# A diffusion backbone on one core: the first feed-forward projection of the second layer by seven products of sums of 2x2 blocks, mixed with the groups of the second projection

## The chip, the cores and the metric

The kernel runs on one core of a Trainium2 chip. The metric is the device time of one execution in microseconds (us), lower is better. The page calls the engines PE (TensorE, matrix products), PEld (its weight loads, which run beside it), DVE (VectorE), ACT (ScalarE), POOL (GpSimd) and SP (SyncE, which here issues transfers). Each engine works off its own instructions in the order in which the program has them, and semaphores hold an instruction back until what it reads is there.

## The reference, cut to what matters

The model has two layers. Each ends with a feed-forward block, and the change touches that of the second layer, in which 512 latent tokens remain (`l == 1`; the first layer also carries 256 context tokens):

```python
def sq_relu_mlp(h, w1, w2):
    return jnp.square(jax.nn.relu(h @ w1)) @ w2
...
    h2 = modulate(rmsnorm(x, g_ff[l]), sh2, sc2)
    x = x + gt2 * sq_relu_mlp(h2, w_ff1[l], w_ff2[l])
```

Here `h` is 512 x 1024, `w1` 1024 x 4096 and `w2` 4096 x 1024, all in 32-bit floats.

## The kernel before

Every 32-bit operand of a product is cut into a high part in the format fp32r and a low part, what is left over (`split`, lines 231 to 242: an ACT copy writes the high part `wh`, line 240; a subtraction, mostly on DVE, writes the low part `wl`, line 241). A product of two such operands takes three matmuls, high by high, high by low and low by high (`mmk`, line 260).

Tokens lie along the free dimension and channels along the 128 partitions. `w_ff1` comes in 32 tiles of 128 output channels, `w_ff2` in 32 tiles of 128 x 1024. The hidden width of 4096 is worked off in eight chunks of 512. In the second layer `ff1_first` computes the first projection of chunk 0 in two halves of 256 tokens; then for c = 1 to 7 `ff1(c)` computes the four tiles of chunk c (each 8 k-steps x 3 matmuls of 512 columns, `f<-h`), `act` applies relu (ACT, line 1226), squares on DVE (line 1228) and splits the result into `fh` and `fl`; and `ff2(c - 1)` runs the second projection of the chunk before: eight groups of 12 matmuls of 512 columns (`f<-fh`, `f<-fl`), one for each output tile `m`, each added into `x[m]` by one DVE instruction (line 1260, `xo<-f`). `ff2_last` does chunk 7 in halves of 256 tokens, and the final norm follows.

Weights come by DMA into `wraw`. `w_get` loads two tiles ahead and splits one tile ahead. Nothing is rescheduled: all engines run in the order in which the code issues instructions, and only background tasks (`spawn`, advanced by `tick`) are mixed in by a clock of estimated PE time. GpSimd takes the subtraction of every eighth weight tile here.

Of the kernel before, what the change touches and what calls it, by code (L numbers as in the profile page):

```python
# [17 lines left out]
DEPTH = 2  # L18
# [44 lines left out]
SLOTS_MIX = {3072: 6, 4096: 4}  # L63


class Slots:
# [46 lines left out]
class Net:  # L113
# [44 lines left out]
    def plan(self):  # L158
        d = self.d
        items = []  # L160

        def win(l, m):
# [12 lines left out]
        def ff1(l, c):  # L175
            for j in range(4):
                items.append((("ff1", l, 4 * c + j), d["w_ff1"][l, 4 * c + j], 1024))

        def ff2(l, c):
            for j in range(4):  # L180
                items.append((("ff2", l, c, j), d["w_ff2"][l, c, j], 1024))

        for l in range(DEPTH):
            for j in range(4):
                items.append((("v", l, j), d["w_v"][l, j], 1024))
            for m in (M_Q, M_K, M_Q + 1, M_K + 1, M_CONV + 2, M_CONV, M_Q + 2, M_K + 2, M_CONV + 3, M_CONV + 1,
                      M_Q + 3, M_K + 3, M_POOL, M_POOL + 1, M_FOUR, M_FOUR + 1):
# [6 lines left out]
            for c in range(1, 8):  # L194
                ff1(l, c)
                ff2(l, c - 1)
            ff2(l, 7)
        self.items = items
        self.n_dma = self.n_split = self.n_got = 0
        self.raw, self.wsp = {}, {}  # L200

    def anywhere(self, i):
        key = self.items[i][0]
# [2 lines left out]
    def w_advance(self, dma, split):  # L206
        nc, sb = self.nc, self.sb
        while self.n_dma < min(dma + 1, len(self.items)):
            i = self.n_dma
            t = sb.get([128, self.items[i][2]], F32, "wraw", self.anywhere(i))  # L210
            nc.sync.dma_start(t, self.items[i][1])
            self.raw[i] = t
            self.n_dma += 1
        while self.n_split < min(split + 1, len(self.items)):
            i = self.n_split
            eng = nc.gpsimd if i % self.pool_share == 0 or i < 4 else nc.vector
            self.wsp[i] = self.split(self.raw[i], "w", ph=self.anywhere(i), eng=eng)
            sb.free(self.raw.pop(i))
            self.n_split += 1

    def w_get(self, *key, split=1, dma=2):
        i = self.n_got
        assert self.items[i][0] == key, (self.items[i][0], key)
        self.n_got += 1
        if split == 1 and not self.in_attention and i + 1 < len(self.items) and self.items[i + 1][0][0] == "br":
            split = 2
        self.w_advance(i, i)
        self.w_advance(i + split, i + split)
        self.w_advance(i + split + dma, i + split)
        return self.wsp.pop(i)  # L230


# [882 lines left out]
    def mixer(self, l, ready, ready_ctx, between):  # L1115
        sb = self.sb
        wide = l < DEPTH - 1
        pairs, attn = [self.values(l, wide, ready, ready_ctx, between)], []
        attention = self.spawn(self.attend(l, wide, pairs, attn, PACE[l]))
        zs, us, up, four, pool, conv = [], [], [], [], [], []  # L1120
        threads = {}
        pairs.append(self.qk(l, 1, wide))
        zs.append(self.conv_in(l, wide, 0))
        pairs.append(self.qk(l, 2, wide))
        zs.append(self.conv_in(l, wide, 1))
        pairs.append(self.qk(l, 3, wide))
        self.pool_in(l, wide, up)
        self.four_in(l, wide, us)

        def attended():  # L1130
            self.join(attention)
            sb.free(*self.v)
            sb.close()
            sb.open(self.tc, SLOTS_MIX)
# [80 lines left out]
    def ff(self, l, ranges, groups, x, h, na, nb, after, near):  # L1215
# [17 lines left out]
        def ff1_first():  # L1233
            ws = [self.w_get("ff1", l, j, split=0 if j < 3 else 1) for j in range(4)]
            banks = [self.bank("f1") for _ in range(4)]
            for k in range(KT):
                self.until(*na, k)
                for w, b in zip(ws, banks):
                    self.mmk(w, 128 * k, h[k], groups[:1], (b,), k == 0, k == KT - 1)
            self.until(*nb, KT - 1)  # L1240
            hid = [act((b,), groups[:1]) for b in banks]
            for w, hl in zip(ws, hid):
                banks = self.proj(w, K8, h, groups[1:], "f1", need=nb)
                sb.free(*w)
                act(banks, groups[1:], hl)
            return hid
# [27 lines left out]
        def ff2_last(hid):  # L1274
# [15 lines left out]
                sb.free(*t)  # L1290
            after(1, ssq, last)

        self.pool_share = SHARES[2 + l]
        hid = ff1_first()
        for c in range(1, 8):
            nxt = ff1(c)
# [365 lines left out]
```

## Time and profile before

| | |
|---|---|
| median of 3 runs | 2151.26 us (2147.72 to 2151.81) |
| the profiled execution | 2151.51 us, of which 2149.7 us are the span on the core |
| PE busy | 2097.2 us, 98% of the span |
| DVE busy | 1378.7 us, 64% |
| ACT busy | 775.2 us, 36% |
| granted TensorE clock, mean | 0.993 |

PE is busy nearly throughout, so the time is read as the sum of PE's matmuls and of the few stretches in which it waits. A busy share of PE says nothing of its pace: matmuls overlap in the records, and the pace is read from where consecutive ones start. For DVE and ACT the share is an average, and what counts is whether a result is there when PE comes to it.

### The profile page before, as it was taken

To read this page: it belongs to the slowest core of one execution; us is meant where nothing else is said; L and a number is where in the kernel's file an instruction comes from. 1 tells how busy PE (TensorE), PEld (TensorE's weight loads), DVE (VectorE), ACT (ScalarE), POOL (GpSimd) and SP (SyncE) were. 2 spreads that over 40 slices of the span, in tenths; PEclk is the share of its full clock that TensorE was granted. 3 is DMA by queue.
4 is the path that set the end of the run, shared out by engine and by line. 5 is a ranking of instruction groups with operands and counts; after the bars stand their busy time and mean duration, and the time that the engine had idled before them with its cause. 6 is when DMAs were issued, how large, how long until landed. Compare 5 with 4: busy or idle time off the path is not lost. (4 is left out here: it accounts for less than half of the span.)

```text
span 2149.7 us, 29024 instructions
## 1 busy us (share of the span) xinstructions
PE 2097.2 (98%) x11700; PEld 1801.3 (84%) x11700; DVE 1378.7 (64%) x2234; ACT 775.2 (36%) x1258; POOL 451.4 (21%) x391
## 2 busy tenths in 40 slices
PE   8899999999999999999999999989999999999998
PEld 6688898888788888888888887878887898888887
DVE  6667658669876559868534365775986465544446
ACT  2455543223443342222112234565333334322333
POOL 2433220015442321212000023333100031000001
PEclk8999999999999999999999999999999999999999
DMA  8111112133344124446321121212332232232221
GB/s 306 44 55 59 55 54 91 50 114 122 118 131 152 71 99 166 165 165 248 109 69 59 60 89 55 69 46 101 121 101 86 98 109 99 97 108 89 88 98 50
DMA packets 62166, 218.36 MB, mean 102 GB/s; under 512 B 7248, under 2 KB 9312, under 8 KB 62032
## 3 DMA queue, kind: packets, MB, share of 16 engines
q1 hardware_dynamic: 45136, 155.21, 21.2%
q0 software_dynamic: 16896, 61.30, 8.3%
q8 instruction: 92, 1.51, 0.3%
q14 instruction: 42, 0.34, 0.0%
HBM read 212.29 MB, written 4.19 MB: 101 GB/s over the span
## 5 line engine op out<-in xcount | busy, mean ns | idle before, releaser
L241 POOL TENSOR_TENSOR wl<-wraw,wh 128x1024 fp32r<-128x1024 f32 x90 | 221.3, 2460 | 1205.2 <-ACT wh L240 956.8
L260 PE MATMUL f<-h,wh 128*128 128x512 f32 (+1 forms) x1600 | 388.7, 349 | 0.0
L260 PEld LDWEIGHTS f<-h,wh 128*128 128x128 f32 x1600 | 264.1, 189 | 41.9
L240 ACT ACTIVATE wh<-wraw 128x1024 fp32r<-128x1024 f32 x268 | 274.2, 1049 | 47.9 <-DVE wl L241 24.0
L241 DVE TENSOR_TENSOR wl<-wraw,wh 128x1024 fp32r<-128x1024 f32 x178 | 243.3, 1371 | 35.6 <-ACT wh L240 33.7
L260 PE MATMUL f<-h,wl 128*128 128x512 f32 (+1 forms) x800 | 243.9, 350 | 0.0
L260 PE MATMUL f<-fh,wh 128*128 128x512 f32 (+1 forms) x800 | 242.8, 349 | 0.0
L260 PE MATMUL f<-fh,wl 128*128 128x512 f32 (+1 forms) x800 | 242.5, 348 | 0.0
L260 PE MATMUL f<-fl,wh 128*128 128x512 f32 (+1 forms) x800 | 242.2, 348 | 0.0
L1260 DVE SCALAR_TENSOR_TENSOR xo<-f,mod,xo 128x512 f32<-128x512 f32 (+1 forms) x200 | 122.9, 640 | 126.7 <-PE f L260 126.6
L1226 ACT ACTIVATE ft<-f 128x512 f32<-128x512 f32 (+1 forms) x100 | 48.0, 510 | 431.5 <-PE f L260 431.5
L321 DVE CUSTOM_DVE_ANT_0 junk<-wm,silu,pp 128x1024 bf16<-128x1024 f32 x116 | 157.7, 1360 | 12.2 <-DMA wm<-w_mod 10.9
L260 PE MATMUL g<-h,wh 128*128 128x512 f32 x512 | 161.3, 393 | 0.0
L1228 DVE TENSOR_TENSOR ft<-ft 128x512 f32<-128x512 f32 (+2 forms) x72 | 54.4, 755 | 166.2 <-ACT ft L1226 166.2
L260 PEld LDWEIGHTS f<-h,wl 128*128 128x128 f32 x800 | 135.5, 189 | 20.7
L260 PEld LDWEIGHTS f<-fh,wh 128*128 128x128 f32 x800 | 134.9, 188 | 21.0 <-issue 0.2
L260 PEld LDWEIGHTS f<-fl,wh 128*128 128x128 f32 x800 | 134.7, 188 | 21.0 <-issue 0.2
L260 PEld LDWEIGHTS f<-fh,wl 128*128 128x128 f32 x800 | 134.7, 188 | 20.7
L260 PE MATMUL g<-hh,wl 128*128 128x512 f32 (+1 forms) x512 | 131.4, 337 | 1.1 <-DVE wl L241 1.1
L260 PE MATMUL g<-hh,wh 128*128 128x512 f32 (+1 forms) x512 | 131.6, 338 | 0.0
L260 PE MATMUL g<-hl,wh 128*128 128x512 f32 (+1 forms) x512 | 131.5, 338 | 0.0
L643 DVE SCALAR_TENSOR_TENSOR ca<-z,pp,ca 128x783 f32<-128x783 f32 (+1 forms) x120 | 121.0, 1009 | 1.9
(401 smaller groups left out, 3905.9 us busy)
## 6 DMA issues: line engine op xcount, KB each, us to landing
wraw<-w_ff SPq DMA_DIRECT2D x128, 512.0 KB, 3.5
wraw<-w_in SPq DMA_DIRECT2D x96, 512.0 KB, 3.5
wm<-w_mod POOLq DMA_DIRECT2D x80, 512.0 KB, 4.5
wm<-w_mod SPq DMA_DIRECT2D x16, 512.0 KB, 10.2
wraw<-w_out SPq DMA_DIRECT2D x16, 512.0 KB, 3.5
wraw<-w_v SPq DMA_DIRECT2D x8, 512.0 KB, 4.9
bias<-bias POOLq DMA_DIRECT2D x16, 256.0 KB, 2.9
wraw<-w_ba SPq DMA_DIRECT2D x8, 512.0 KB, 3.8
```

Of the source, the lines that this page charges most:

```text
L240: nc.scalar.activation(hi, src, AF.Copy)
L241: (eng or nc.vector).tensor_tensor(lo, src, hi.bitcast(F32), op=OP.subtract)
L260: self.nc.tensor.matmul(o[:, :t1 - t0], a[:, sl], b[:, t0:t1], start=start and a is wh and b is xh, stop=stop and a is wl)
L321: nc.vector.tensor_tensor_reduce(self.junk, w, self.silu[c], 1.0, b, OP.mult, OP.add, o)
L643: nc.vector.scalar_tensor_tensor(a[:, :n], zs[ct][:, j:j + n], w, a[:, :n], op0=OP.mult, op1=OP.add)
L1226: nc.scalar.activation(t[:, a - a0:e - a0], o[:, :e - a], AF.Relu)
L1228: nc.vector.tensor_tensor(t, t, t, op=OP.mult)
L1260: nc.vector.scalar_tensor_tensor(x[m][:, a:e], o[:, :e - a], self.modcol(l, int(a >= SEQ), 5, m), x[m][:, a:e], op0=OP.mult, op1=OP.add)
```

## The change

In the second layer the first projection of 13 of the 16 pairs of weight tiles (pairs 3 to 15; pairs 0 and 1 are chunk 0, and pair 2 stays as it was) is computed in another way. Weights of a pair and tokens are both cut in 2x2 blocks (two halves of the 1024 input channels by two output tiles, and by two halves of the 512 tokens). Instead of eight block products there are seven, P1 to P7, of sums and differences of blocks (Strassen's scheme in Winograd's form). Each product is 12 matmuls of 256 columns. The sums of the token side (T1 to T4) are formed once (`sums`), those of the weight side for every pair (`seven_weights`), and the results are combined while they leave the accumulators (`seven`, `square`). `ff_order` lays out by a fixed rule which product or second-projection group comes next, and `w_ahead` issues weight splits for all that comes within 6 us of PE time by that list, and loads for 12 us.

```diff
+SLOTS_MIX = {3072: 6, 4096: 4}, {3072: 2, 4096: 7}
+STRASSEN = (1,)
+PLAIN_PAIRS = 3
+SEVEN = "P1", "P6", "P7", "P5", "P2", "P4", "P3"
+SPLIT_US, LOAD_US, FF_LEAD = 6.0, 12.0, 5.6
...
+            for q in (2 * c, 2 * c + 1):
+                if q < PLAIN_PAIRS:
+                    a += [("plain", 2 * q + i, 0, 24 * us) for i in range(2)]
+                else:
+                    a += [("seven", q, j, 6 * us) for j in range(7)]
+            b = deque(("add", c - 1, m, 12 * us) for m in range(8))
+            total, more, ta, tb = sum(s[3] for s in a), sum(s[3] for s in b), 0.0, 0.0
+            for s in a:
+                while b and (ta - FF_LEAD) / (total - FF_LEAD) > (tb + 6 * us) / more:
+                    out.append(b.popleft())
+                    tb += 12 * us
+                out.append(s)
+                ta += s[3]
+            out += b
...
+        name = SEVEN[j]
+        if name == "P1":
+            src = a
+        elif name == "P6":
+            st["s1"], st["s2"] = (sb.get([128, 512], F32, "ws", ph=True) for _ in range(2))
+            nc.vector.tensor_tensor(st["s1"], c, e, op=OP.add)
+            src = st["s2"]
+            nc.vector.tensor_tensor(src, st["s1"], a, op=OP.subtract)
+        elif name == "P7":
+            src = c
+            nc.vector.tensor_tensor(src, a, c, op=OP.subtract)
...
+        else:
+            src = st["s1"]
+            nc.vector.tensor_tensor(src, b, st["s2"], op=OP.subtract)
+        w = sb.get([128, 2, 512], F32R, "w7", ph=True)
+        self.split(src, "w7", w[:, 0], w[:, 1])
...
+            for k in range(4):
+                v = sb.get([128, 4, 256], F32, "v7", ph=True)
+                for i in range(2):
+                    hi, lo = (t[:, :512].bitcast(F32).rearrange("p (a b) -> p a b", a=2) for t in h[k + 4 * i])
+                    nc.vector.tensor_tensor(v[:, 2 * i:2 * i + 2], hi, lo, op=OP.add)
+                    yield 0.7
+                for o, a, b in ((0, 1, 0), (1, 3, 1), (3, 3, 0), (2, 2, 3)):
+                    nc.vector.tensor_tensor(v[:, o], v[:, a], v[:, b], op=OP.subtract)
+                yield 1.0
...
+                    blocks[n].append(self.split(v[:, i], "T7", hi, lo))
+                    yield 0.6
...
+            b1, o1 = product(0)
+            nc.scalar.activation(u, o1, AF.Copy)
+            yield
+            b6, o6 = product(1)
+            nc.vector.tensor_tensor(u, o6, u, op=OP.add)
...
+            product(5)
+            nc.vector.tensor_tensor(t1[:, 0], o7, u, op=OP.add)
+            ps.free(b7)
+            nc.scalar.activation(t1, t1, AF.Relu)
+            square(t1, hid[1])
+            yield
+            product(6)
+            nc.vector.tensor_tensor(t0[:, 1], o5, u, op=OP.add)
+            ps.free(b5)
+            nc.scalar.activation(t0[:, 1], t0[:, 1], AF.Relu)
+            square(t0, hid[0])
...
+        def square(t, hl):
+            f = t.rearrange("p a b -> p (a b)")
+            nc.scalar.activation(f, f, AF.Square)
+            self.split(f, "f", hl[0], hl[1])
```

The order of the steps that `ff_order` gives for chunks 2 to 7 is the same each time: P1, P6, P7, P5, P2 of the first pair, add 0, P4, add 1, P3, then of the second pair P1, add 2, P6, add 3, P7, add 4, P5, add 5, P2, P4, add 6, P3, add 7 ("add m" is the second projection's group for output tile m, of the chunk before).

PE, in chunk 1, before: a tile of the first projection is 24 matmuls of 512 columns, of which these six are two k-steps (`h` with an odd number is the high part, with an even number the low part).

```order
L260 MATMUL f_1457_16119<-h_15603,wh_16075 128x512
L260 MATMUL f_1457_16119<-h_15604,wh_16075 128x512
L260 MATMUL f_1457_16119<-h_15603,wl_16076 128x512
L260 MATMUL f_1457_16119<-h_15605,wh_16075 128x512
L260 MATMUL f_1457_16119<-h_15606,wh_16075 128x512
L260 MATMUL f_1457_16119<-h_15605,wl_16076 128x512
```

PE, with the change, in chunk 2: the second half of product P6, from columns of `h` set aside for a token sum and the weight sum `w_3444`, and the first matmuls of group add 3.

```order
L1441 MATMUL f_1496_16684<-h_15615,w_3444_16619 128x256
L1441 MATMUL f_1496_16684<-h_15616,w_3444_16619 128x256
L1441 MATMUL f_1496_16684<-h_15615,w_3444_16619 128x256
L1441 MATMUL f_1496_16684<-h_15617,w_3444_16619 128x256
L1441 MATMUL f_1496_16684<-h_15618,w_3444_16619 128x256
L1441 MATMUL f_1496_16684<-h_15617,w_3444_16619 128x256
L364 MATMUL f_1498_16698<-fh_16078,wh_16611 128x512
L364 MATMUL f_1498_16698<-fl_16079,wh_16611 128x512
```

A product is half as wide as a matmul before, and first- and second-projection groups now alternate within a chunk.

DVE, over one chunk's end and the next one's start, before: the last two additions into `x`, then weight tiles `wl` alternate with the squaring (`ft`) and the low part (`fl`) of a finished tile.

```order
L1260 SCALAR_TENSOR_TENSOR xo_15446<-f_1473_16297,mod_103,xo_15446 128x512
L1260 SCALAR_TENSOR_TENSOR xo_15477<-f_1475_16311,mod_103,xo_15477 128x512
L241 TENSOR_TENSOR wl_16326<-wraw_16261,wh_16325 128x1024
L1228 TENSOR_TENSOR ft_16358<-ft_16358 128x512
L241 TENSOR_TENSOR fl_16357<-ft_16358,fh_16356 128x512
L241 TENSOR_TENSOR wl_16364<-wraw_16295,wh_16363 128x1024
```

DVE, with the change, at the same place: the combination after P4 (`ft_17064`) and the low part of its square, add 6 (`xo_15446`), the low part of the next P1's weights (`w_3581`), the two sums and the low part for P6 (`ws`, `w_3584`), the combination after P3 (`ft_17063`) and its low part, add 7 (`xo_15477`), and the difference (`wraw_17207`) and low part for the next P7 (`w_3607`).

```order
L1465 TENSOR_TENSOR ft_17064<-f_1532_17135,u_3552_17065 128x256
L345 TENSOR_TENSOR fh_17062<-ft_17064,fh_17061 128x512
L1364 SCALAR_TENSOR_TENSOR xo_15446<-f_1540_17239,mod_103,xo_15446 128x512
L345 TENSOR_TENSOR w_3581_17253<-wraw_17205,w_3581_17253 128x512
L294 TENSOR_TENSOR ws_17256<-wraw_17207 128x512
L296 TENSOR_TENSOR ws_17257<-ws_17256,wraw_17205 128x512
L345 TENSOR_TENSOR w_3584_17260<-ws_17257,w_3584_17260 128x512
L1471 TENSOR_TENSOR ft_17063<-f_1535_17169,u_3552_17065 128x256
L345 TENSOR_TENSOR fh_17060<-ft_17063,fh_17059 128x512
L1364 SCALAR_TENSOR_TENSOR xo_15477<-f_1543_17282,mod_103,xo_15477 128x512
L299 TENSOR_TENSOR wraw_17207<-wraw_17205,wraw_17207 128x512
L345 TENSOR_TENSOR w_3607_17304<-wraw_17207,w_3607_17304 128x512
```

The weights of the next chunk's first products now stand behind the combinations and additions of the chunk that ends.

ACT, with the change, over the same stretch: relu, square and high part of P4's result (`ft_17064`, `fh_17061`), the high parts for the next P1 and P6, relu, square and high part of P3's result, and the high part for P7.

```order
L1467 ACTIVATE ft_17064<-ft_17064 128x512
L1480 ACTIVATE ft_17064<-ft_17064 128x512
L344 ACTIVATE fh_17061<-ft_17064 128x512
L344 ACTIVATE w_3581_17253<-wraw_17205 128x512
L344 ACTIVATE w_3584_17260<-ws_17257 128x512
L1473 ACTIVATE ft_17063<-ft_17063 128x256
L1480 ACTIVATE ft_17063<-ft_17063 128x512
L344 ACTIVATE fh_17059<-ft_17063 128x512
L344 ACTIVATE w_3607_17304<-wraw_17207 128x512
```

Before, ACT had one relu and one high part for a finished tile, with DVE's squaring between them; now three ACT instructions follow each other between DVE's combination and DVE's low part.

## Rows read from the trace of the kernel before

**Rows 1.** The page's head, and the last chain (start us, us, what; matmuls counted).

```profile
span 2149.7 us, 29024 instructions
PE 2097.2 (98%) x11700; PEld 1801.3 (84%) x11700; DVE 1378.7 (64%) x2234; ACT 775.2 (36%) x1258; POOL 451.4 (21%) x391
...
1799.99 329.38 PE f L260 x1508
```

**Rows 2.** Windows: one chunk of the second layer's feed-forward, and a stretch of halves.

```profile
core 0: us, PE busy (x) PEld busy (x) DVE busy (x) ACT busy (x) POOL busy (x), PEclk, DMA share, GB/s
1849.32:1893.70 44.38, 44.38 (x195) 36.30 (x194) 21.75 (x24) 12.53 (x16) 2.40 (x1) 1.00 0.29 95
...
2116.00:2120.00 4.00, 4.00 (x36) 4.00 (x35) 2.42 (x5) 1.79 (x3) 0.00 (x0) 1.00 0.00 0
```

**Rows 3.** Timeline of PE: start us, us, what, count. Starts of groups give the pace.

```profile
1827.12 0.39 PE L260 MATMUL f<-fh,wh 128*128 128x512 f32 x1
...
1849.32 0.61 PE L260 MATMUL f<-h,wh 128*128 128x512 f32 x2
...
2114.96 0.28 PE L260 MATMUL f<-fh,wh 128*128 128x256 f32 x1
...
2120.65 0.27 PE L260 MATMUL f<-fh,wh 128*128 128x256 f32 x1
```

**Rows 4.** Groups of instructions, chunks 1 to 7: busy us, mean ns, idle before.

```profile
L240 ACT ACTIVATE wh<-wraw 128x1024 fp32r<-128x1024 f32 x58 | 57.8, 1045 | 0.0
L1260 DVE SCALAR_TENSOR_TENSOR xo<-f,mod,xo 128x512 f32<-128x512 f32 x55 | 41.2, 749 | 57.3 <-PE f L260 57.3
L241 DVE TENSOR_TENSOR fl<-ft,fh 128x512 fp32r<-128x512 f32 x28 | 19.4, 693 | 19.6 <-ACT fh L240 19.6
L240 ACT ACTIVATE fh<-ft 128x512 fp32r<-128x512 f32 x28 | 17.7, 633 | 21.2 <-DVE ft L1228 21.2
L241 DVE TENSOR_TENSOR fl<-ft,fh 128x256 fp32r<-128x256 f32 x1 | 0.4, 426 | 0.5 <-ACT fh L240 0.5
L240 ACT ACTIVATE fh<-ft 128x256 fp32r<-128x256 f32 x1 | 0.4, 418 | 0.5 <-DVE ft L1228 0.5
```

**Rows 5.** Timeline of DVE and of ACT in chunk 2.

```profile
1855.62 0.69 DVE L1228 TENSOR_TENSOR ft<-ft 128x512 f32<-128x512 f32 x1 [4.21 <-ACT ft L1226]
1857.01 0.69 DVE L241 TENSOR_TENSOR fl<-ft,fh 128x512 fp32r<-128x512 f32 x1 [0.70 <-ACT fh L240]
...
1874.60 1.23 DVE L241 TENSOR_TENSOR wl<-wraw,wh 128x1024 fp32r<-128x1024 f32 x1 [0.26 <-ACT wh L240]
1875.74 0.74 DVE L1260 SCALAR_TENSOR_TENSOR xo<-f,mod,xo 128x512 f32<-128x512 f32 x1
...
1856.34 0.63 ACT L240 ACTIVATE fh<-ft 128x512 fp32r<-128x512 f32 x1 [0.76 <-DVE ft L1228]
1856.88 1.05 ACT L240 ACTIVATE wh<-wraw 128x1024 fp32r<-128x1024 f32 x1
```

**Rows 6.** Timeline of PE: three of its waits, and what followed the longest.

```profile
1408.13 0.39 PE L915 MATMUL S<-qk,qw 128*128 128x256 f32 x1 [2.08 <-DVE PTl L967]
...
733.28 1.12 PE L428 MATMUL rstd<-diag,ones 128*128 128x512 f32 x2 [2.52 <-DVE diag L422]
...
1767.96 0.70 PE L428 MATMUL rstd<-diag,ones 128*128 128x256 f32 x2 [3.27 <-DVE diag L422]
1768.31 0.58 PE L260 MATMUL o<-br,wh 128*128 128x256 f32 x2
...
1772.10 0.45 PE L260 MATMUL o<-br,wh 128*128 128x256 f32 x2
```

**Rows 7.** Windows after three of those waits (columns as in Rows 2).

```profile
735.50:737.50 2.00, 2.00 (x11) 2.00 (x11) 1.87 (x2) 1.17 (x2) 2.00 (x2) 0.50 0.00 0
1408.20:1410.20 2.00, 2.00 (x11) 1.74 (x12) 1.04 (x5) 1.29 (x3) 0.00 (x0) 1.00 0.48 131
1770.00:1772.00 2.00, 2.00 (x11) 2.00 (x11) 1.86 (x1) 0.51 (x2) 2.00 (x1) 0.50 0.00 0
```

More of the change, by code (lines that the diff above doesn't have):

```diff
@@ L160, in plan @@
         items = []
+        self.when, self.sevens = {}, {}
         def win(l, m):
@@ L193, in plan @@
             ff1(l, 0)
-            for c in range(1, 8):
-                ff1(l, c)
-                ff2(l, c - 1)
+            if l in STRASSEN:
+                t = 0.0
+                for kind, a, b, us in self.ff_order(l):
+                    if kind == "plain":
+                        items.append((("ff1", l, a), d["w_ff1"][l, a], 1024))
+                    elif kind == "seven":
+                        items.append((("seven", l, a, b), d["w_ff1"][l, 2 * a + b] if b < 2 else None, 1024))
+                    elif b % 2 == 0:
+                        items.append((("ff2", l, a, b // 2), d["w_ff2"][l, a, b // 2], 1024))
+                    self.when[items[-1][0]] = self.when.get(items[-1][0], t)
+                    t += us
+            else:
+                for c in range(1, 8):
+                    ff1(l, c)
+                    ff2(l, c - 1)
             ff2(l, 7)
@@ L200, in plan, with ff_order @@
         self.raw, self.wsp = {}, {}
+    @staticmethod
+    def ff_order(l):
+        w = NTOK if l < DEPTH - 1 else SEQ
+        us = w / 2217.0
+        out = []
+        for c in range(1, 8):
+            a = []
+            for q in (2 * c, 2 * c + 1):
[12 more added lines that the diff above has]
+            out += b
+        return out
     def anywhere(self, i):
@@ L229, in w_get, with seven_weights, w_ahead, until @@
         self.w_advance(i + split + dma, i + split)
+        return self.wsp.pop(i)
+    def seven_weights(self, i, l, q, j):
+        nc, sb = self.nc, self.sb
+        st = self.sevens.setdefault((l, q), {})
+        if j < 2:
+            st["raw", j] = self.raw.pop(i)
+        a, b = (st["raw", 0][:, 512 * k:512 * k + 512] for k in range(2))
+        if j:
+            c, e = (st["raw", 1][:, 512 * k:512 * k + 512] for k in range(2))
+        name = SEVEN[j]
[9 more added lines that the diff above has]
+            nc.vector.tensor_tensor(src, a, c, op=OP.subtract)
+        elif name == "P5":
+            src = st["s1"]
+        elif name == "P2":
+            src = b
+        elif name == "P4":
+            src = e
+        else:
+            src = st["s1"]
+            nc.vector.tensor_tensor(src, b, st["s2"], op=OP.subtract)
+        w = sb.get([128, 2, 512], F32R, "w7", ph=True)
+        self.split(src, "w7", w[:, 0], w[:, 1])
+        if name == "P4":
+            sb.free(st["raw", 1])
+        if name == "P3":
+            sb.free(st["raw", 0], st["s1"], st["s2"])
+        return w
+    def w_ahead(self, *key):
+        i = self.n_got
+        now = self.when[key]
+        def until(us):
+            j = i
+            while j + 1 < len(self.items) and self.when.get(self.items[j + 1][0], now + us + 1.0) <= now + us:
+                j += 1
+            return j
+        split, load = max(until(SPLIT_US), i + 1), until(LOAD_US)
+        self.n_got += 1
+        assert self.items[i][0] == key, (self.items[i][0], key)
+        self.w_advance(i, i)
+        self.w_advance(split, split)
+        self.w_advance(max(load, split + 1), split)
         return self.wsp.pop(i)
@@ new lines, in square, with mixed @@
+        def square(t, hl):
+            f = t.rearrange("p a b -> p (a b)")
+            nc.scalar.activation(f, f, AF.Square)
+            self.split(f, "f", hl[0], hl[1])
+        def mixed():
+            hid = ff1_first()
+            t7 = self.spawn(sums())
+            nxt, gen = [], None
+            for kind, a, b, _ in self.ff_order(l):
+                if kind == "plain":
+                    w = self.w_ahead("ff1", l, a)
+                    banks = self.proj(w, K8, h, ranges, "f1")
+                    sb.free(*w)
+                    nxt.append(act(banks, ranges))
+                elif kind == "seven":
+                    if b == 0:
+                        self.join(t7)
+                        pair = [tuple(sb.get([128, SEQ], F32R, "fh", ph=True) for _ in range(2)) for _ in range(2)]
+                        nxt += pair
+                        gen = seven(a, pair)
+                    next(gen)
+                else:
+                    if b % 2 == 0:
+                        w2 = self.w_ahead("ff2", l, a, b // 2)
+                    ff2_one(a, b, w2, hid, ranges)
+                    if b % 2:
+                        sb.free(*w2)
+                    if b == 7:
+                        for t in hid:
+                            sb.free(*t)
+                        hid, nxt = nxt, []
+            for t in h:
+                sb.free(*t)
+            sb.free(*x7["keep"])
+            return hid
```

66 lines of the change are left out of this document (61 added, 5 removed).

## Prediction, written before the changed kernel ran

> **What bounds the kernel now.** The page comes first: PE is busy for 98% of the span and the chain that ended last is one unbroken run of feed-forward matmuls [rows 1]. Next come the windows over the second layer: a chunk of the feed-forward takes 44.3 us, PE is busy through all of it at a granted clock of 1.00, DVE is busy for 21.75 us of it and ACT for 12.5 [rows 2]. So this part is as long as PE's matmuls, and the two engines that prepare operands have about half their time free. The timeline gives PE's pace: from 1827.12 to 1849.32 lie 96 matmuls of 512 columns, 231 ns each; from 2114.96 to 2120.65 lie 48 of 256 columns (four groups of 12), 118.5 ns each [rows 3].
>
> **What the change takes off PE.** A pair of tiles is 2 x 24 = 48 matmuls of 512 columns, 48 x 0.2308 = 11.08 us. Seven products of 12 matmuls of 256 columns are 84 x 0.1185 = 9.95 us. That is 1.12 us for a pair and **14.6 us** for 13 pairs, if PE never waits.
>
> The weight loads rise from 48 to 84 for a pair. In the 256-column stretch PEld is busy without a break, yet the matmuls start every 118.5 ns [rows 2, 3]: the load is hidden there, and I charge nothing for it. [...]
>
> **What it puts on DVE and ACT.** Prices from rows: a DVE instruction of 512 columns 0.69 us, of 256 0.43, an addition into `x` 0.75; an ACT pass of 512 columns 0.63, of 256 0.42, of 1024 1.05 [rows 4]. If the next instruction waits for nothing it starts 0.08 to 0.09 us before the end, so that in a row DVE gives 0.61, 0.67 (addition) and 1.14 (weight tile of 1024) and ACT 0.54; a hand-over from DVE to ACT takes 0.03 and back 0.04 [rows 5]. No row has a combination that reads an accumulator at 256 columns; I take 0.43, bounded by 0.35 (0.43 in a row) and the 0.75 of an addition twice as wide.
>
> Per chunk of two pairs DVE has 14 low parts (8.5), 8 weight sums (5.2, some waiting for each other), 10 combinations (4.0), 4 low parts of results (2.4), 4 weight tiles (4.6) and 8 additions (5.4): 30.1 us. DVE works in order, and behind some of these it stands until ACT is through, with everything behind it: P6, P7 and P3 form a sum, ACT copies it, DVE subtracts (0.70 each); P4's result goes through three ACT passes before its low part (3 x 0.63 and hand-overs, 2.0), P3's through three as well (1.8). Per pair 5.9, per chunk 11.8. So DVE is taken up for 42 us, and PE's work in a chunk is 2 x 9.95 + 96 x 0.231 = 42.05. There is no slack left: any bunching makes PE wait, and the weights of all of the next seven steps stand behind it in DVE's queue.
>
> **Where it bunches.** I walk the rows of the order from a point at which DVE is idle and waits for PE, the end of add 5. From there DVE has to do, before PE can start the next chunk's P7: the addition (0.2 after PE's end, 0.67), a weight tile (1.14), P3's sum, ACT and low part (0.69, 0.70, 0.61), P4's combination, ACT and low part (0.43, 2.02, 0.61), addition (0.67), P1's low part (0.61), P6's two sums, ACT and low part (0.69, 0.72, 0.70, 0.61), P3's combination, ACT and low part (0.43, 1.81, 0.61), addition (0.67), P7's difference and ACT (0.69, 0.66). With 0.1 for PE to take it up this is **16.0 us**. PE meanwhile has P2, P4, add 6, P3, add 7, P1 and P6: 5 x 1.42 + 2 x 2.77 = **12.6 us**. So PE waits 3.4 us before each P7 of a chunk's first pair, and 0.5 in it for the low part. The lead of 6 us doesn't help, because it counts PE's clock at which DVE is to be handed the work, not when DVE reaches it.
>
> From the end of add 0 the same walk gives add 2's weights after 8.5 us (addition, P3's sum, ACT, two low parts, combination, 2.02 of ACT, low part, addition, weight tile), where PE comes to their low part after P4, add 1, P3, P1 and two matmuls, 7.5: 1.0. Then P6 of the second pair waits 0.2, and P7 1.3 (0.8 and 0.5). Sum per period: 3.9 + 1.0 + 0.2 + 1.3 = 6.4 us, a period of **48.5 us** against 44.3 before. Between add 0 of chunk 2 and add 0 of chunk 7 lie five periods: 32.2 us. After it chunk 7 still has 2.5, and the last groups wait some 1.5 for the result of the last P3.
>
> **The first chunk with the new products.** The token sums stand in DVE's queue in four bundles: 2 additions of 512 columns, 4 differences and 4 low parts of 256, some 4.6 us each, 18.5 together. Before P6 of pair 3 has its low part DVE must work off these, three weight tiles (3.4), the squares of pair 2 (2.6), three additions (2.0), P1's low part (0.6) and P6's sums (2.0): 29.1 us, and waits for ACT of about 3.8, from 1.9 us after the chunk's start (that is when `ff1_first` leaves DVE): **34.8 us**. PE is there after 11.08 + 4 x 2.77 + 1.42 and two matmuls = 23.8. So 11.1 us of waiting lie ahead of this point, most of it in one piece. The rest of the chunk, up to the first P7 of chunk 2, adds 5 more. Bounds: nothing, if the sums had been done in DVE's free time, and 18.5 plus that 5 if none of them were.
>
> **The clock.** [...] From 1768.31 to 1772.10 lie 18 matmuls of 256 columns in 3.79 us in place of 2.13: 1.66 us lost [rows 6]. Seven of the waits above are longer than 2.52 (one before P6 of pair 3, six before the first P7 of a chunk): 7 x 1.66 = 11.6 us.
>
> **The sum.** Waits 11.1 + 5 + 32.2 + 2.5 + 1.5 = 52.3; the clock 11.6; less 14.6: +49.3 us. The profiled execution took 2151.5, which is also within 0.3 us of the median: **2201 us**. GpSimd takes fewer weight tiles than before and loads are issued 12 us ahead, with DMA busy for 0.29 of a chunk [rows 2]; both I take as hidden, and a load late by its lead would show as DVE waiting for a DMA.
>
> **Rivals.**
> - *The lead covers it, faster.* The place is the stretch from add 5 to P7. If DVE's work and waits there come to at most 12.6 us in place of 16.0, a fifth less, DVE is there first and stays there; the token sums then fall into the 22 us that DVE has free in a chunk. Then PE only saves: 2151.5 - 14.6 = 2137. For it speaks that DVE's busy share alone, 30 of 42 us, is well below full; against it that the pauses for ACT are as plain in the trace as the work (0.70 in each `fl` [rows 5]). Chance 0.18.
> - *PE waits as worked out, but the clock holds or the waits are half as long.* The waits of 3.4 need only shrink by 0.9 to come to the row of 2.52. Without the clock's part it gives 2189, with half of the waits as well 2163. Chance 0.20.
> - *Hardly any difference*, with some 15 us of waits that eat up the saving: 2151, chance 0.04.
> - *DVE and ACT are slower than alone, or loads come late too*: 2215 to 2235, chance 0.06.
>
> The forecast itself has 0.52, and by it alone the time is 2185 to 2215. The range takes in the second rival and half of the first: **2142 to 2224**. What a measurement of this kernel can tell from no change is about 0.2%, 4.3 us. Faster by more than that 0.18, within it 0.04, slower 0.78.
>
> **What would show it.** Right: seven products take 9.95 us where PE doesn't wait, matmuls of the products start every 118 to 119 ns; a chunk lasts about 48 us in place of 44.3, with PE waiting 3 to 4 us for ACT's high part or DVE's difference before the first P7 of each chunk and about 7 us before P6 of pair 3; the granted clock is 0.50 behind those waits; DVE's longest waits are for ACT inside the squares. Wrong: chunks of 42 us with PE busy throughout (the lead covers it); waits of PE for DMA; or products slower than 118.5 ns a matmul, which would put the fault into PE's own price.

## The result: 2199.95 us, 2.3% slower, and the profile after

The changed kernel took 2199.95 us (median of 4 runs, 2198.52 to 2200.96), the kernel before beside it on the same chip 2150.82 (2147.72 to 2151.81): a ratio of 1.0230, 95% interval 1.0213 to 1.0248. The head of its page:

```profile
span 2198.8 us, 30361 instructions
PE 2110.1 (96%) x12168; PEld 1829.9 (83%) x12168; DVE 1451.1 (66%) x2434; ACT 829.9 (38%) x1391; POOL 441.3 (20%) x387
```

Against [rows 1] PE is now busy for 96% and no longer for 98%, and DVE has 72 us more to do. What follows calls *the walk* the stretch in which the second projection is mixed with the first, from the first tile after `ff1_first` to the first tile of `ff2_last`. Before it went from 1805.06 to 2114.96 us, now from 1800.51 to 2161.92. Its windows, cut at the first P7 of a chunk (columns as in [rows 2]):

```profile
1862.55:1912.54 49.99, 45.19 (x264) 39.62 (x264) 30.51 (x49) 20.21 (x35) 0.00 (x0) 0.97 0.31 95
...
2064.88:2116.00 51.12, 46.44 (x264) 40.86 (x264) 30.51 (x49) 20.20 (x35) 0.00 (x0) 0.93 0.21 72
2116.00:2161.92 45.92, 43.36 (x240) 38.01 (x241) 27.96 (x41) 18.07 (x31) 2.35 (x1) 0.93 0.21 69
...
1800.51:2161.92 361.41, 322.04 (x1814) 280.72 (x1813) 226.44 (x361) 142.51 (x246) 7.09 (x3) 0.95 0.24 79
```

A chunk takes 50 to 51 us in place of 44.4 [rows 2]; DVE is busy for 30.5 of them, and PE's clock is 0.93 to 0.97 and no longer 1.00. What PE waits for in the walk (us in total, times, longest):

```profile
PE f L1441 <- ACT w L344: 28.5, 13, 6.0
PE f L1441 <- DVE w L345: 3.7, 10, 1.7
PE f L364 <- DVE wl L345: 3.5, 5, 0.8
PE f L364 <- POOL wl L345: 3.4, 2, 1.7
```

It is the weights of the products, their high part from ACT (`w` L344) above all. The chain that ended last shows why they are late. From the addition behind add 5 to the first P7 of the next chunk it runs through DVE and ACT alone (start us, us, what; "issue" pieces left out):

```profile
2049.03 0.06 DVE xo L1364
...
2052.98 0.35 DVE ft L1465
...
2053.35 0.64 ACT ft L1467
...
2054.02 0.64 ACT ft L1480
...
2054.68 0.64 ACT fh L344
...
2055.96 0.74 DVE xo L1364
...
2060.02 0.35 DVE ft L1471
...
2060.39 0.43 ACT ft L1473
...
2060.84 0.64 ACT ft L1480
...
2061.50 0.64 ACT fh L344
...
2062.16 0.69 DVE fh L345
2062.85 0.66 DVE xo L1364
2063.51 0.61 DVE wraw L299
...
2064.20 0.64 ACT w L344
...
2064.88 1.31 PE f L1441 x3
```

`ft L1465` and `ft L1471` are the combinations behind P4 and P3. After each, DVE stands until ACT has done relu, square and copy; `wraw L299`, the difference that P7 needs, is queued behind both stops. It depends on neither.

On PE's timeline the wait, what follows it, and the smaller wait before the second pair's P7:

```profile
2013.79 3.23 PE L1441 MATMUL f<-T,w 128*128 128x256 f32 x12 [3.19 <-ACT w L344]
2016.82 4.42 PE L1441 MATMUL f<-h,w 128*128 128x256 f32 x24
2021.07 0.62 PE L364 MATMUL f<-fh,wh 128*128 128x512 f32 x2
...
2038.90 0.39 PE L364 MATMUL f<-fh,wl 128*128 128x512 f32 x1
2039.82 0.50 PE L1441 MATMUL f<-T,w 128*128 128x256 f32 x2 [0.54 <-ACT w L344]
2040.55 1.46 PE L1441 MATMUL f<-T,w 128*128 128x256 f32 x10 [0.22 <-DVE w L345]
2041.84 0.63 PE L364 MATMUL f<-fh,wh 128*128 128x512 f32 x2
```

P7's 12 matmuls take 3.03 us from start to start and the 24 of P5 and P2 4.25, where 118.5 ns a matmul [rows 3] makes 1.42 and 2.84: the clock is down (0.61 granted over the 8 us from 2013.80 on, see fill below). And a wait costs more than the idle time in brackets: from 2038.90, one matmul (0.23) and P7 (1.42) would bring PE to 2040.55; it gets to 2041.84, 1.29 us later, where the brackets hold 0.76. So the walk is added up below from starts.

### The profile page after: what moved, and what is told of

Its sections match the earlier page's. It is cut to its first block, busy times and chain, and to the rows that moved or that the text cites. A ratio compares the mean times of both kernels' runs of the same rounds, so it can differ in the third digit from the quotient of the medians.

```text
span 2198.8 us, 30361 instructions
## 1 busy us (share of the span) xinstructions
PE 2110.1 (96%) x12168; PEld 1829.9 (83%) x12168; DVE 1451.1 (66%) x2434; ACT 829.9 (38%) x1391; POOL 441.3 (20%) x387
## 5 line engine op out<-in xcount | busy, mean ns | idle before, releaser
L364 PE MATMUL f<-fh,wh 128*128 128x512 f32 (+1 forms) x1040 | 289.2, 353 | 0.9 <-ACT fh L344 0.4
L344 ACT ACTIVATE wh<-wraw 128x1024 fp32r<-128x1024 f32 x242 | 249.5, 1048 | 48.4 <-DVE wl L345 23.1
L364 PE MATMUL f<-h,wh 128*128 128x256 f32 (+1 forms) x1184 | 257.7, 333 | 0.0
L345 DVE TENSOR_TENSOR wl<-wraw,wh 128x1024 fp32r<-128x1024 f32 x156 | 202.5, 1304 | 32.7 <-ACT wh L344 30.9
L364 PEld LDWEIGHTS f<-h,wh 128*128 128x128 f32 x1184 | 184.7, 188 | 24.2
L364 PEld LDWEIGHTS f<-fh,wh 128*128 128x128 f32 x1040 | 173.3, 188 | 26.3 <-ACT fh L344 0.7
L425 DVE CUSTOM_DVE_ANT_0 junk<-wm,silu,pp 128x1024 bf16<-128x1024 f32 x116 | 157.7, 1360 | 12.3 <-DMA wm<-w_mod 11.0
L364 PE MATMUL f<-h,wl 128*128 128x512 f32 (+1 forms) x592 | 161.8, 335 | 0.0
L364 PE MATMUL f<-fl,wh 128*128 128x512 f32 (+1 forms) x560 | 155.2, 342 | 0.0
L1186 ACT ACTIVATE g<-g 128x512 f32<-128x512 f32 x96 | 46.9, 523 | 194.2 <-PE g L364 193.3
L364 PE MATMUL y<-br,wh 128*128 128x512 f32 x480 | 119.6, 357 | 0.3 <-DVE br L345 0.2
L1441 PEld LDWEIGHTS f<-h,w 128*128 128x128 f32 x780 | 108.4, 206 | 12.8 <-ACT w L344 6.5
```

The lines of the kernel that those rows point to most:

```text
L344: nc.scalar.activation(hi, src, AF.Copy)
L345: (eng or nc.vector).tensor_tensor(lo, src, hi.bitcast(F32), op=OP.subtract)
L364: self.nc.tensor.matmul(o[:, :t1 - t0], a[:, sl], b[:, t0:t1], start=start and a is wh and b is xh, stop=stop and a is wl)
L425: nc.vector.tensor_tensor_reduce(self.junk, w, self.silu[c], 1.0, b, OP.mult, OP.add, o)
L1186: nc.scalar.activation(g[:, a:e], o[:, :e - a], func, scale=scale)
L1441: nc.tensor.matmul(o, y, x_, start=fresh and k + i == 0, stop=k == 3 and i == 2, skip_group_check=True)
```

## The experiments

The theory, from the prediction: DVE works in order, and the weights that PE needs next stand behind its stops for ACT and behind the token sums; the long waits then cost clock as well. Rivals: DVE's and ACT's work of a chunk is as long as PE's in any order; products are slower when mixed; the loss of clock falls into waits that come anyway.

All kernels, from their profiles: where the walk starts, how long it is, and what follows it up to the end of the span (us), beside the median time.

| kernel | walk starts | walk | behind it | time | ratio to before (95%) |
|---|---|---|---|---|---|
| before | 1805.06 | 309.9 | 34.7 | | |
| the change | 1800.51 | 361.4 | 36.9 | 2199.95 | 1.0213 to 1.0248 |
| lead8 | 1805.39 | 330.3 | 48.1 | 2183.66 | 1.0135 to 1.0169 |
| late_low | 1807.87 | 345.1 | 47.4 | 2200.32 | 1.0211 to 1.0246 |
| no_sums | 1799.78 | 348.5 | 37.3 | 2189.99 | 1.0167 to 1.0197 |
| fill | 1798.71 | 352.7 | 36.9 | 2190.85 | 1.0175 to 1.0205 |
| lead8_own | 1804.82 | 329.1 | 36.1 | 2172.29 | 1.0091 to 1.0122 |
| lead8_plain4 | 1807.38 | 318.5 | 36.0 | 2162.03 | 1.0042 to 1.0070 |
| pe_only | 1798.24 | 296.5 | 36.0 | 2132.91 | 0.9911 to 0.9938 |
| head_dve | 1802.86 | 309.9 | 34.7 | 2149.58 | 0.9991 to 1.0008 |
| lead10_plain4 | 1801.94 | 327.6 | 36.1 | 2168.84 | 1.0077 to 1.0104 |
| paced_plain4 | 1804.06 | 324.7 | 36.2 | 2166.71 | 1.0060 to 1.0087 |
| late8_paced | 1805.48 | 314.1 | 36.5 | 2158.29 | 1.0026 to 1.0053 |
| mended | 1805.33 | 309.1 | 36.5 | 2152.24 | 1.0000 to 1.0018 |

**PE alone (pe_only).**

```diff
-                        items.append((("seven", l, a, b), d["w_ff1"][l, 2 * a + b] if b < 2 else None, 1024))
+                        items.append((("seven", l, a, b), d["w_ff1"][l, 2 * a] if (a, b) == (PLAIN_PAIRS, 0) else None, 1024))
...
+        if not self.sevens:
+            w = self.sevens[0] = sb.get([128, 2, 512], F32R, "w7", ph=True)
...
+        return self.sevens[0]
```

> One prepared pair of weight parts serves all products: the loads, sums and splits of the other weights and the token sums are left out (so this kernel computes neither). PE's order, its 12,168 matmuls and the combinations stay. It prices the change on PE alone: 13 pairs x 1.12 = 14.6 us less than 2150.8, and 0 to 4.5 us from the head of the block: 2131 to 2137 us. By the rival that products of 256 columns, mixed with the second projection, run slower than the 118.5 ns a matmul read before, the time is above 2141.

2132.91 us. PE waits nowhere in the walk, and the granted clock is 1.00 throughout. A period from one chunk's first product to the next chunk's is 41.96 to 42.35 us, 42.18 in the mean of five (1841.41 to 2052.32), and the walk is 13.4 us shorter than before. The products cost nearly what was predicted; what the change loses, it loses by waiting for operands and by the slower clock behind the waits.

**The place in DVE's queue (lead8).**

```diff
-SPLIT_US, LOAD_US, FF_LEAD = 6.0, 12.0, 5.6
+SPLIT_US, LOAD_US, FF_LEAD = 8.0, 14.0, 5.6
...
-SLOTS_MIX = {3072: 6, 4096: 4}, {3072: 2, 4096: 7}
+SLOTS_MIX = {3072: 6, 4096: 4}, {1024: 1, 2048: 4, 3072: 1, 4096: 6}
```

> The weights of a product are prepared for up to 8 us of PE time ahead instead of 6 (loads 14 instead of 12; the slots of the phase are cut smaller to hold the extra buffer). DVE's queue then has the sum for the first pair's P7 ahead of the second pair's P3 combination, with the 1.8 us that DVE stands for ACT behind it. By the theory that the place in DVE's queue makes the waits of 3.2 us at six first P7, they shrink to 0 to 0.5 us and TensorE keeps 1.00 there, which gives back 6 x (3.2 + 1.6) = 29 us less up to 3: 2171 to 2175 us. By the rival that VectorE's and ScalarE's work of a chunk (30 us and its stops) is as long as PE's whatever its order, another product waits in its place, and the time stays within 4 us of 2200.

2183.66, between the two. But the walk is 31.1 us shorter: the six waits of 3.2 us are gone, and from chunk 2 on 0.6 and 0.96 at P5 are what is left (1.2 and 0.96 in one chunk). The walk bears out the theory, with the same work on DVE (226.4 us in both walks). DVE also stands for ACT as long as it did; what fell is the time that it stands for PE. The changed kernel and lead8, each in its walk (us in total, times, longest):

```profile
DVE fh L345 <- ACT fh L344: 48.1, 25, 2.0
DVE xo L1364 <- PE f L364: 45.3, 21, 4.1
...
DVE fh L345 <- ACT fh L344: 48.1, 25, 2.0
DVE xo L1364 <- PE f L364: 18.0, 18, 2.1
```

So in the changed kernel DVE and PE stand for each other in turn, and the work of neither alone is the limit. The other half was lost again outside it: 11.2 us behind the walk, 4.9 ahead of it. At the end of the kernel ACT's squares now stood for the output's transfers:

```profile
2157.95 0.42 ACT L544 ACTIVATE sq<-xo 128x256 f32<-128x256 f32 x1 [0.86 <-DMA out_dram<-out]
...
2161.61 0.42 ACT L544 ACTIVATE sq<-xo 128x256 f32<-128x256 f32 x1 [2.69 <-DMA out_dram<-out]
```

**Whose fault the end is (lead8_own).**

```diff
-            _, _, pool, tags = min(fit, key=lambda a: a[:2])
+            spare = len(self.pools) > 1 and self.total is SLOTS_MIX[1] and name not in ("u7", "ft", "ws")
+            _, _, pool, tags = min(fit, key=lambda a: (spare and a[0] < 3072, *a[:2]))
```

> As lead8, but the small slots are kept for the tiles of the products; others take them only when nothing else is free. In lead8 the squares of the last norm all had the one 1 KB slot, so that each square stood for the GpSimd addition of the one before: the end from the first tile of the last groups on took 48.1 us in place of 36.9. By the theory that this is the slots' doing and not the lead's, 10.5 us come back at the end and up to 5 before the walk (whose first plain tile began at 1805.4 in place of 1800.5): 2168 to 2174 us. By the rival that the longer lead itself costs this (it moves DVE's work to where it hurts), the time stays near 2184.

2172.29, and 36.1 us behind the walk: the slots' doing. The smallest slot that fits was the only one of 1 KB, and it passed between squares and outputs, so that (not quite as the expectation had it) each square stood for an output's transfer. The start of the walk stayed 4.3 us late.

**Fewer stops by a later low part (late_low).**

```diff
-            self.split(f, "f", hl[0], hl[1])
+            nc.scalar.activation(hl[0], f, AF.Copy)
+            late.append(lambda: nc.vector.tensor_tensor(hl[1], f, hl[0].bitcast(F32), op=OP.subtract))
```

> The subtraction that makes the low part of a squared result is issued on DVE one step later, behind the next evacuation, so that DVE stands less for ACT's three passes; all else as in the change, the slots cut smaller. By the theory of the queue, each of the two stops per pair shrinks by the 0.7 us evacuation that now stands ahead and by what PE's progress hides: the first P7's weights come 2.5 us sooner, the six waits of 3.2 us fall to about 0.7. If TensorE then keeps 1.00 the time is 2200 - 6 x 2.5 - 6 x 1.6 = 2175 us, if it still drops to 0.50 2185. By the rival that the sum of DVE's and ACT's work limits, DVE's busy time of a chunk is unchanged (30 us) and so is the period of 51.1 us: 2200.

2200.32, no gain, by the table for the same reason as lead8: the walk is 16.3 us shorter (5 of the six waits at P7 fell to 1.8 us, one to 0.9), and 10.5 behind it and 7.4 ahead of it ate this up. The time is the rival's, but not its period: from first P7 to first P7 it is 47.0 to 49.1 us in place of 50 to 51. The 1.8 us are more than expected: P3's low part is still ahead of P7's difference and still stands 1.16 us for ACT.

**The token sums (no_sums).** `T1` to `T4` are replaced by blocks that are there already.

```diff
-                for o, a, b in ((0, 1, 0), (1, 3, 1), (3, 3, 0), (2, 2, 3)):
-                    nc.vector.tensor_tensor(v[:, o], v[:, a], v[:, b], op=OP.subtract)
...
+            for n, m in (("T1", "B11"), ("T2", "B21"), ("T3", "B22"), ("T4", "B11")):
+                blocks[n] = blocks[m]
```

> The eleven token-block sums per 256 features, their splits and their rebuilding of the high and low parts are left out: the products read plain blocks in place of the four sums (so this kernel does not compute the token sums). By the theory that the token sums hold up pair 3, its waits (1.65 and 6.02 at P6, 0.5 at a low part, about 2.5 more) and its half clock go, the later six waits of 3.2 us stay: 2200 - 11 - 1.7 = 2185 to 2190 us. By the rival that the weights' preparation alone makes chunk 1 wait, P6 of pair 3 waits as long as before and the time stays within 3 us of 2200.

2189.99, at the upper end; the walk is 12.9 us shorter. All waits of 0.4 us or more up to the first P7 of chunk 2 are gone, and that one stays at 3.30, the later ones at 3.1.

**The clock (fill).**

```diff
+                fill = 36 if (q, n) == (3, "P6") else 14 if q % 2 == 0 and n == "P7" else 0
...
+                        nc.tensor.matmul(spare[:, W], h[0][0][:, :128], h[0][0][:, W], start=True, stop=True)
```

> PE is kept busy over the waits with 36 matmuls of 256 columns into a spare bank before P6 of pair 3 and 14 before each first-pair P7 (added work, whose results nobody reads). They take 14 x 0.118 = 1.7 us of a wait of 3.2 us, so they delay nothing. By the theory that the wait makes TensorE's clock drop to half for the next 3 us, the clock stays at 1.00 behind each and 7 x 1.6 = 11 us come back: 2189 us. By the rival that the clock's loss falls into waits that follow anyway, the time stays within 2 us of 2200.

2190.85: 9.1 us back, for added work. Windows of 8 us behind the seven long waits of the changed kernel:

```profile
1833.40:1841.40 8.00, 7.99 (x35) 7.33 (x36) 5.13 (x8) 3.94 (x6) 0.00 (x0) 0.65 0.01 2
1862.50:1870.50 8.00, 7.73 (x44) 7.22 (x45) 4.90 (x8) 3.16 (x6) 0.00 (x0) 0.79 0.37 107
...
2013.80:2021.80 8.00, 8.00 (x40) 7.65 (x41) 4.62 (x7) 3.09 (x6) 2.38 (x1) 0.61 0.21 66
2064.90:2072.90 8.00, 8.00 (x39) 7.66 (x40) 4.86 (x8) 3.08 (x6) 0.00 (x0) 0.61 0.00 0
2116.00:2124.00 8.00, 8.00 (x39) 7.67 (x40) 4.89 (x8) 3.11 (x6) 0.00 (x0) 0.60 0.20 66
```

With the two windows left out (0.79 each) that is 8 x (0.35 + 3 x 0.21 + 2 x 0.39 + 0.40) = 17.3 us lost. With the filler three of the seven still show 0.79, 5.0 us, and four 1.00. So 12.3 us of clock came back and the walk got 8.7 shorter: the other 3.6 went into longer waits, as the rival had it for all of it. A period in which the clock held, 2009.20 to 2057.86, lasts 48.66 us.

**More time for the sums (lead8_plain4).** `PLAIN_PAIRS = 4` in place of 3.

> As lead8_own, with four pairs of tiles computed in full in place of three: the token sums have one pair's 11.1 us more before a product needs them. PE pays 1.1 us for the pair. By the theory that chunk 1 waits for the token sums behind DVE's other work, its waits of 1.6, 4.1 and 1.8 us at pair 3 and the half clock behind them go: 8 to 9 us less 1.1, so 7 us under lead8_own, 2161 to 2167. By the rival that the first seven weights of the walk are what comes late, the same waits come one pair later, and the time is 1 us over lead8_own.

2162.03, 10.3 under lead8_own. The waits at pair 3 (1.64, 4.06, 1.53) are gone; a new one of 1.93 stands at a full tile ahead of it, behind the sums.

**A longer lead yet, and slower sums (lead10_plain4, paced_plain4).** The first sets `SPLIT_US, LOAD_US = 10, 16` and the slots to `{1024: 2, 2048: 4, 3072: 2, 4096: 5}`; the second also doubles the steps of the token sums, `yield 1.4`, `2.0` and `1.2` in place of 0.7, 1.0 and 0.6.

> As lead8_plain4 with the weights up to 10 us ahead (loads 16), two 3 KB slots and two 1 KB slots in the place of one 4 KB slot. DVE's queue then has the weights of the walk's P5 too ahead of the P3 combination. By the theory of the place in the queue the last waits of a chunk, 0.55 and 0.97 us at P5, go in five chunks: 7.6 us under lead8_plain4, with 0 to 4 us from the slots before the walk: 2150 to 2155 us. By the rival that VectorE and ScalarE together now set the pace, a wait of that size comes back at another product, and the time stays at 2160 to 2164.

> As lead10_plain4, with the token sums handed to DVE at half the pace: with four full pairs they are not wanted before chunk 2, and in lead8_plain4 PE waited 0.4 to 1.9 us five times (4.1 us, and 1.7 us of half clock) for the weights of full tiles that stood behind sums in a stretch where DVE was busy 18.8 of 20 us. By the theory that the place of the sums in DVE's queue makes these waits they go: 5 to 6 us under lead10_plain4, 2144 to 2150, at or under the kernel before. By the rival that DVE has no room before chunk 2 either, the waits come later with the same sum: no change against lead10_plain4.

Both missed, at 2168.84 and 2166.71, the first above its rival's range too. P5 waits no longer, but P2 does, for something new: the copy `u` of P1's bank, which must be read before P2 adds to it. It stands in ACT's queue (lead10_plain4):

```profile
1949.60 0.63 ACT L1481 ACTIVATE ft<-ft 128x512 f32<-128x512 f32 x1
1950.26 0.63 ACT L345 ACTIVATE fh<-ft 128x512 fp32r<-128x512 f32 x1
1950.80 1.04 ACT L345 ACTIVATE wh<-wraw 128x1024 fp32r<-128x1024 f32 x1
1951.75 0.61 ACT L345 ACTIVATE w<-wraw 128x512 fp32r<-128x512 f32 x1
1952.27 0.36 ACT L1449 ACTIVATE u<-f 128x256 f32<-128x256 f32 x1
...
1952.68 2.93 PE L1442 MATMUL f<-h,w 128*128 128x256 f32 x12 [2.81 <-ACT u L1449]
```

P1 was through before 1946.6, but ACT was still with the passes of P3's result and with copies of weights that are wanted only later. The two copies hold `u` up by 1.5 us (from 1950.80 to 1952.27) of the 2.81 that P2 waits. A lead that is too long does on ACT what one that is too short did on DVE. The slower sums took the first mixed chunk's waits away, as expected (0.53, 2.75 and 0.54), and put 2.66 and 0.62 at the walk's first products, so that little was won: there they came too late.

**Both ways together, and mended.** `late8_paced` is late_low with a lead of 8, four full pairs, the paced sums and lead8_own's rule for small slots.

> Four full pairs and paced sums, with a lead of 8 us in place of 10 and the low parts of the squared results one step later. It tells whether the two ways of getting DVE past its stops for ACT do the same: by the theory of the place in the queue this one leaves a part of the 1.5 us at P5 in each of five chunks (the weights of P5 still stand behind the P3 combination, though no longer behind its stop of 1.8 us): 2146 to 2154 us. By the rival that only the longer lead helps, it has lead8_plain4's waits at P5 and is 5 us or more above paced_plain4.

2158.29, above the theory's range, and 8.4 under paced_plain4 where the rival had it 5 or more above. P5 waits 1.12 to 1.18 us for ACT and 0.3 for DVE in each of five chunks, and beside it only the walk's first products (0.62 and 1.77). So P5 waits as long as in lead8_plain4 (0.53 to 0.60 and 0.97 there), as the rival had it, and a chunk without loss of clock takes 44.17 us here (from 1902.42 to 1946.59) and 44.30 there (from 2042.20 to 2086.50): with a lead of 8 the later low part brings the chunks next to nothing. Of the 4.4 us by which the walk is shorter than lead8_plain4's, 2.7 lie ahead of the first of these waits. `mended` adds

```diff
-        split, load = max(until(SPLIT_US), i + 1), until(LOAD_US)
+        more = 1.5 if key[0] == "seven" and key[3] == 6 and key[2] % 2 else 0.0
+        split, load = max(until(SPLIT_US + more), i + 1), until(LOAD_US)
```

token sums at two thirds of their first pace, and the slots of lead10_plain4, in which small tiles take turns.

> As late8_paced, with three further edits: at the last product of a chunk the weights' lead is 1.5 us longer, so that the copy and subtraction for the next P5 (on ScalarE ahead of the P3's relu, on DVE ahead of its combination) come before the stop, and no later weight does (in lead10_plain4 ScalarE had a weight copy too many ahead of the copy that frees P1's bank, and P2 waited 1.2 to 2.8 us); the token sums run at two thirds of their first pace in place of half; small tiles of the norm take turns in more slots. By the theory of the place in the queue, the five waits at P5 (1.15 and 0.3 us) and the waits at the walk's first products (0.6 and 1.8 us, 1.7 of half clock) of late8_paced go, 0 to 4 us come back ahead of the walk: 2145 to 2153 us, level with the kernel before. By the rival that DVE and ScalarE have no room left, other products wait, and the time stays at 2156 to 2160.

2152.24 us, a ratio of 1.0000 to 1.0018: level with the kernel before, as expected, and not for quite the reason. P5 and the first products wait no longer and the clock is 1.00 through the walk, but P2 waits for `u` in five chunks:

```profile
2034.05 1.69 PE L1444 MATMUL f<-h,w 128*128 128x256 f32 x12 [1.54 <-ACT u L1451]
```

Between the passes of P3's result and `u` two weight copies still stand on ACT, from 2032.17 to 2033.63. So the one wait of P5 was exchanged for another of its size, which is the rival's picture at this one place. The walk is 309.1 us, 12.6 above pe_only's, 1.1 of them for the fourth full pair; it starts at 1805.33, without the shorter head of the changed kernel.

**The head of the block (head_dve).** The change made the walk start 4.55 us sooner, which no step of the prediction had. In the kernel before a DVE operation on two columns took 2.40 us there. The edit, on the kernel before:

```diff
+            if self.items[i][0] == ("ff1", 1, 4):
+                eng = nc.vector
```

> The kernel before the change, with one edit: the low part of the fifth tile's weight, which GpSimd computes at 1780.14 us beside the norm's tiny DVE operations, goes to DVE. By the theory that a two-column DVE operation took 2.40 us (0.16 elsewhere) because GpSimd's subtraction ran beside it, PE's wait of 3.05 us and the slow clock behind it shrink: 3 to 4.5 us less, 2146 to 2148. By the rival that DVE is late there for another reason, the 1.2 us more on DVE change nothing or cost up to 1 us: 2151 to 2152.

2149.58 against 2149.47 beside it: no difference. The operation took 0.16 us again, but DVE's own subtraction (1.23) now stood ahead of it, and it had stood 2.60 us for ACT's copy, which waited for the tile's transfer; PE waited 3.20 us in place of 3.05. So this run doesn't price the 2.40 us. The traces of the kernel before and of the changed kernel do, at the norm's matmul that PE waits for:

```profile
1785.50 0.91 PE L428 MATMUL rstd<-diag,ones 128*128 128x256 f32 x2 [3.05 <-DVE diag L422]
...
1782.48 0.70 PE L532 MATMUL rstd<-diag,ones 128*128 128x256 f32 x2 [0.33 <-DVE diag L526]
...
1782.24 2.43 POOL L345 TENSOR_TENSOR wl<-wraw,wh 128x1024 fp32r<-128x1024 f32 x1 [3.89 <-ACT wh L344]
```

In the changed kernel ACT's copy of the same tile waits for its transfer until 1781.10 in place of 1779.00, so GpSimd's subtraction begins 2.1 us later, behind the norm's operations, and these take their 0.16 us. PE's wait is 2.72 us shorter, and the stretch at a clock of 0.50 that followed it in the kernel before (0.54 granted from 1785.60 to 1789.20, against 1.00 from 1782.60 to 1786.60) is not there, which makes 1.53 from this matmul to the walk's start (19.56 us before, 18.03 now); 0.3 lay ahead. That is the 4.55 us. They come from when one load landed, and not from the products: in no_sums, fill and pe_only PE waits the same 0.33 us there. Why the load landed later is not followed up here.

## Why the prediction was right, and which terms were not

2201 us was forecast, 2199.95 measured. Every term against the profile, in us (the spans differ by 49.1):

| term | predicted | measured |
|---|---|---|
| PE's work | -14.6 | -13.4 (pe_only) |
| first mixed chunk, waits | 16.1 | 13.2 = 62.04 - 46.0 (pe_only) - 2.8 of clock |
| five periods, waits | 32.2 | 31.3 = 253.45 - 210.91 (pe_only) - 11.3 of clock |
| chunk 7, waits | 2.5 | 3.1 = 45.92 - 39.6 (pe_only) - 3.2 of clock |
| clock | 11.6 | 17.3 |
| last groups | 1.5 | 2.1 |
| head of the block | 0 | -4.6 |
| sum | 49.3 | 49.1 |

- **PE and its weight loads.** Right, with 12 matmuls of a product in 1.42 us where nothing waits; the charge of nothing for a weight load ahead of each held in pe_only, where PE waits for none of the products' 1,092 matmuls and 60 of them, from 1841.41 to 1848.53, take 118.7 ns each. The saving was 1.2 us less than forecast: a period of pe_only is 42.18 us in the mean, where 42.05 was worked out. (The 0.2308 us of the sum isn't what its rows give, 22.20 / 96 = 0.2313; over 13 pairs that is 0.3 us.)
- **The walk from add 5 to P7.** Worked out as 16.0 us; the chain has 2064.88 - 2049.03 = 15.85, and the 0.2 ahead of the addition that the walk began with. The order of the steps was that of the queue, each stop of 2.0 and 1.8 us for ACT as priced (2.03 and 1.81), and so the waits: 3.2 at P7, 0.7 to 0.8 at add 2 (1.64 and 1.74 where GpSimd had the low part), 0.76 recorded and 1.29 from start to start at the second pair's P7. A period without loss of clock, 48.66 us in fill, was put at 48.5. Chunk 7 is longer than forecast for one of GpSimd's two low parts, which the prediction had taken as hidden: the group waited 1.74 for it.
- **That no slack is left.** This was the step's wording for DVE's 42 us, and it went too far. lead8 has the same work and the same stops for ACT (48.1 us), and its P5 waits 1.5 us of a chunk where the changed kernel's PE stands some 5: the stops are not work that must be done, they only hold up what is queued behind them. The rival that the lead covers it failed for a lead of 6 us by 3.2 us, and for one of 8 by 1.5.
- **Token sums.** 16.1 against 13.2: the piece before P6 was 1.65 and 6.02 us, with 0.15 and 0.54 beside, less than the 11.1 worked out. no_sums and lead8_plain4 show the cause.
- **The clock.** The seven places were right, and that the clock falls to 0.50 behind each. That all waits longer than 2.52 us would lose clock was my estimate from three waits of [rows 6, 7]; no run shows the 11.6 us that it gave, the windows under fill show 17.3. The price was not right: I took 1.66 us for each from one row. Three of the seven cost 1.7, one 2.8, three 3.1 to 3.2.
- **The last groups.** They waited 0.45 and 0.34 us for the last P3, half of the 1.5. The rest of the 2.1 is another thing: pe_only, where no such wait is recorded, is some 1.2 us longer than the kernel before there too.
- **The head and the clock** were off by 4.6 and 5.7 us, in opposite directions, and the first mixed chunk by 2.9 in the head's. That the sum is within 1.1 us is luck; that the waits of the five periods came at the forecast places with 31.3 us against 32.2 is not.

## What to carry to other kernels

A change that takes work off the engine that sets the pace is worth its saving only if what it puts on the others arrives in time; add up their queues in order, with each stop for a third engine, and not their busy shares: DVE was busy for 60% of a chunk and stood for PE for 45 us of the walk, and PE still waited over 3 us in each chunk. Before asking for less work, look whether what is wanted next is queued behind a stop on which it doesn't depend, and shift it by just that much, since a lead that is too long does the same harm on the next engine. And when an edit needs other buffers, read the stretches that it shouldn't touch: here one small slot cost 11 us at the far end of the kernel.

## What the runs showed of the hardware

Waits of equal length did not cost the same clock here. Behind 3.35, 3.15 and 3.17 us of waiting the clock was at 0.50 for some 3.4 us, behind 3.19, 3.20 and 3.19 for some 6.3 (the windows under fill). They also differ in when the clock fell: in the long ones it was down 0.4 to 0.6 us before PE started again, in the short ones it fell 0.4 to 1.7 us after. One of each, the window ahead of the start at 2013.79 and that behind the start at 1963.63:

```profile
2013.20:2013.75 0.55, 0.00 (x0) 0.00 (x0) 0.00 (x0) 0.55 (x2) 0.00 (x0) 0.50 0.00 0
...
1963.65:1965.35 1.70, 1.48 (x10) 1.27 (x11) 1.70 (x3) 1.70 (x4) 0.00 (x0) 1.00 0.00 0
```

A wait under 2.08 us, the longest with 1.00 behind it in [rows 6, 7], could cost clock too. In late_low five waits at P7 are equally long, 1.79 to 1.82 us. Behind three of them the 36 matmuls of P7, P5 and P2 took 6.17 to 6.38 us up to the start of the next group (from 2013.60 to 2019.77, for one), behind two 4.87 (from 1966.58 to 1971.45); at 118.5 ns each they make 4.27. P7's 12 from 2013.60 took 3.03 us, as those from 2013.79 did in the changed kernel at a granted clock of 0.50. So the length of a wait alone didn't tell what it cost.

DVE's operations on two columns in the changed kernel's norm took 0.16 or 0.17 us (from 1779.58 to 1781.96, with no GpSimd instruction beside them). In the kernel before, one that began 0.03 us after GpSimd's subtraction took as long as that, 2.40 us:

```profile
1780.09 0.17 DVE L381 TENSOR_SCALAR n10hv<-nv 128x2 f32<-128x2 f32 x1
1780.17 2.40 DVE L383 TENSOR_SCALAR n10y<-nv 128x2 int32<-128x2 int32 x1
...
1780.14 2.40 POOL L241 TENSOR_TENSOR wl<-wraw,wh 128x1024 fp32r<-128x1024 f32 x1 [2.15 <-ACT wh L240]
```

In late_low such an operation took 2.34 us beside a subtraction of 2.41, in lead8 2.03 beside one of 2.38. In all three it ended 0.02 to 0.03 us after GpSimd's. What held it up no trace shows.
